# Diagonal copies onto ScalarE, one score buffer for all heads, scans cut at the chunks, and a new hand-written order for the four heads of an HGRN2 block

## The chip, the cores and the metric

The kernel runs on one core of a Trainium2 chip. The measure is device time in microseconds of one execution. Engines are named as in the profile: PE is TensorE (matmul), PEld its weight loads, DVE VectorE, ACT ScalarE, POOL GpSimd, SP SyncE (here only an issuer of DMAs). Each engine works through its own queue in the order in which the program was written out; semaphores make it wait for others.

## The reference

One decoder layer over 16 meta tokens and 1024 tokens, model width 1024, everything in float32. The mixer runs a gated linear recurrence (HGRN2, four heads of key and value width 128) beside a pooling branch; a gated MLP follows. Only the recurrence is touched by the change.

```python
def hgrn2(q, f_logit, i, g, lb, out_gain):
    f = lb + (1.0 - lb) * jax.nn.sigmoid(fl)
    log_f = jnp.log(jnp.maximum(f, LOG_FLOOR))
    k = (1.0 - lb) * jax.nn.sigmoid(-fl)
    ...
def _hgrn2_chunk_step(state, xs):
    b = jnp.cumsum(lf, axis=2)
    o_inter = jnp.einsum('bhtk,bhkv->bhtv', q * jnp.exp(b), state)
    diff = b[:, :, :, None, :] - b[:, :, None, :, :]
    decay = jnp.where(causal, jnp.exp(jnp.where(causal, diff, 0.0)), 0.0)
    scores = jnp.einsum('bhtk,bhtsk,bhsk->bhts', q, decay, k)
    o_intra = jnp.einsum('bhts,bhsv->bhtv', scores, v)
    ...
def reference(...):
    u = rmsnorm(h, mix_norm_pre[l])
    proj = u @ w_in[l]
    q, f_logit, i_in, g_out, v_pool, gate_a, gate_b = jnp.split(proj, cuts, axis=-1)
    a = hgrn2(q, f_logit, i_in, g_out, lbs[l], hgrn_out_norm[l])
    p = multiscale_pool(v_pool, pool_proj[l], pool_scale[l])
    z = (sigmoid(gate_a) * (a @ w_branch_hgrn[l]) + sigmoid(gate_b) * (p @ w_branch_pool[l]))
    h = h + rmsnorm(z @ w_out[l], mix_norm_post[l])
    ...  # gated MLP
```

The cumulative sum `b` starts anew at each chunk; the kernel uses chunks of 128 tokens behind a first one of 16 meta tokens.

## The kernel before

The time has four stretches. From 0 to about 250 us the input is normed and transposed and the merge gates are projected. From about 250 to 585 us come the heads, the pooling branch and the branch products (called the head stage here). Then come the output projection and the MLP, to the end at 1333 us.

**Arithmetic on PE.** A float32 matrix product is made from three products of parts: weights are cast to a high part (`whi`, ACT, L156) and the rest is subtracted into `wlo` (L157, on DVE or POOL). A projection job of the head stage (F the forget gate, Q the query, G the output gate, PV the pooling values, each for one head) is 72 matmuls of some 346 columns. BB and BA are the branch products of half that length.

**One head.** When F's product is there, ACT writes two sigmoids from PSUM (`post_f`, L629 and L630). Step c (`chain_f`) then makes the log gate: two ACT scalings (L634, L635), two DVE clamps (L636, L637), two ACT logarithms (L638, L639), an addition (`lf`, L640), and the cumulative sum `b` by a scan along 1040 columns (L641). The scan multiplies the running sum by `keep_on`, an array of ones with a zero at the start of each chunk. `head_steps` then runs in steps, one for each "h" in the order.

- Scores are made by levels 2, 4, 8, 16, 32, 64, two of them in a step. A level subtracts `b` from its middle value of each block (`sub`, L686), takes two exponentials on ACT (L688, L689), multiplies by `q` and by `kk` (`lq`, L690; `lk`, L691) into a tile `d`, and PE makes 32 or fewer small products into the PSUM tile `sl` (L708, or L702 for levels 32 and 64).
- Levels 2 to 16 go by a masked DVE copy (L724) into `dg`, a narrow array of 128 x 256, in which each group of 32 partitions holds its own 32 x 32 diagonal block of each of the 8 chunks. Levels 32 and 64 are copied by DVE straight into `sc`, the full score array of 128 x 1024 (L718).
- A later step makes the base of the diagonal blocks on PE (`sb`, L777), joins it into `dg` (L780), and copies the four groups of 32 partitions of `dg` onto the diagonal of `sc` (L788; `dg0` to `dg3`).
- Between them stand the decayed keys (`kd`: L745, L746, L750), the decayed queries (`qs`: L741, L751), the chunk decays `ebl` (L748), the products of odd steps (`e1q`, L758; `e1k`, L759), the transposes of `kd` (`pt`, L766, copied out by ACT at L767), the states (`ds`, L801; L804 on DVE) and the outputs (`po`).

**What sets the order.** `ORDER` is the sequence of jobs and steps written by hand: `F1` is a job, `Fa3` and `Fb3` its halves, `c1` the log gate chain, `h1` the next step of head 1, `sp`, `sa` and `w` splits and weight work. A scheduler then interleaves matmuls more finely within it. `POOLED` names the operations that POOL does instead of DVE (`lq32.1` is L690 of level 32 of head 1, `wQ0` the weight subtraction of job Q0), `ACTED` those that ACT does.

At the end of the head stage, DVE multiplies the gates into the branch products out of PSUM (L918), and `split_z` (L1172 to L1177) prepares the output projection, whose weights POOL splits at L1265.

Of the kernel before, what the change touches and what calls it, by code (L numbers as in the profile page):

```python
# [8 lines left out]
F32 = mybir.dt.float32  # L9
# [3 lines left out]
ALU = mybir.AluOpType  # L13

P = 128
D = 1024
SEQ = 1024
NM = 16
L = SEQ + NM
# [14 lines left out]
HEADS = 4  # L34
NCH = 8
# [8 lines left out]
BLK = 32  # L44
# [5 lines left out]
EARLY_G = 2  # L50
SUMS_AT = {5: (2,), 6: (2, 1), 8: (3,), 9: (1, 3), 10: (1, 4), 11: (4, 0), 12: (0, 0)}
FM_SLOTS = 26
LP = 1056
U0 = LP - L
NRAW = 3
ZA = 4
AHEAD = 3

ORDER = ("F0 c0 Q0 h0 F1 h0 h0 c1 Q1 h0 h1 h0 F2 h1 h1 c2 h0 h0 Q2 h1 h2 G2 h1 h0 h2 h0 Fa3 h1 h0 h1 h2 Fb3 h2 c3 "
# [3 lines left out]
POOLED = ("e1k.3 kdmul.2 kdmul.3 lk32.1 lk4.1 lq16.1 lq32.1 lq32.2 lq64.0 lq64.3 lq8.0 lq8.1 lq8.2 osg.2 sub2.2 "  # L63
          "sub32.1 sub8.1 wBA2 wBA6 wBA7 wBB2 wF0 wF2 wF3 wPP2 wPV0 wPV1 wQ0 wQ1 lq4.3 kdsub.1 qsmul.1 lk32.0 e1q.3 "
          "e1q.1 lq2.1 wQ2 sub2.3 rsl.0 lk32.3 qsmul.2 dg1.3").split()
ACTED = ("").split()
TRUNC = False

CH_ALL = [(0, 348), (348, 346), (694, 346)]
# [4 lines left out]
def trunk_kernel(ctx: ExitStack, tc: tile.TileContext, x, meta_tokens, mix_norm_pre,  # L74
# [4 lines left out]
    act, dve, pool_e, pe = nc.scalar, nc.vector, nc.gpsimd, nc.tensor  # L79

    cnt = [0]
    const = ctx.enter_context(tc.tile_pool(name="const", bufs=1))
# [21 lines left out]
    def slot(n, dtype=F32, name="s"):  # L104
        return stage["fm", "p"].tile([P, n], dtype, tag="fm", name=nm(name), padded_shape=[P, LP])

    def ubig(dtype, name, n=KD * LP):
        return upool.tile([P, n], dtype, tag="u", name=nm(name), padded_shape=[P, KD * LP])

# [13 lines left out]
    def small(shape, name, tag, bufs=4):  # L123
        return sm.tile(shape, F32, tag=tag, name=nm(name), bufs=bufs)
# [7 lines left out]
    open_pool("ps", 8, PSUM)  # L132


    eps_t = const.tile([P, 1], F32, name="eps_t")
    dve.memset(eps_t, EPS)
    act.activation(small([P, 1], "std", "ns"), eps_t, AF.Sqrt)
    ident = const.tile([P, P], F32, name="ident")
    make_identity(nc, ident)
    onesm = const.tile([P, P], F32, name="onesm")  # L140
    pool_e.memset(onesm, 1.0 / P)
    onesr = const.tile([P, P], F32R, name="onesr")
    pool_e.tensor_copy(onesr, onesm)
# [76 lines left out]
    class Strassen:  # L220
# [3 lines left out]

        ORDER = ("P1", "P2", "P6", "P5", "P3", "P7", "P4")
        MOVING = dict(P1="b11", P2="b21", P3="b22", P4="t4", P5="t1", P6="t2", P7="t3")
        SECOND = ("P3", "P5", "P7")

        def __init__(self, units, run, early, quarters, halo, put, whole):
# [6 lines left out]
            for u in run:  # L236
                self.seq += [(u, p) for p in self.ORDER if u >= early or p not in ("P1", "P2")]
            self.got, self.at, self.kept, self.begun = [], 0, [], {}
# [333 lines left out]
                dve.tensor_copy(um[:, :, NM:], rr(ulo[:, :, :NM]))  # L572

    vd = dram.tile([NCH, P, 512], F32, name="vscr")
    vmeta = const.tile([P, 512], F32, name="vmeta")

    um = slot(2 * NM * KD, F32R, "um").rearrange("p (k c) -> p k c", k=KD)
# [43 lines left out]
    def eng(op):  # L621
        return pool_e if op in POOLED else dve

# [9 lines left out]
    def chain_f(h, kk, b, f, f2):  # L633
        act.activation(f2, f, AF.Identity, scale=omlu[:, h : h + 1], bias=lbu[:, h : h + 1])  # L634
        act.activation(f, f, AF.Identity, scale=oml[:, h : h + 1], bias=lb[:, h : h + 1])  # L635
        dve.tensor_scalar(f2, f2, 1.0, LOG_FLOOR * LUP, ALU.min, ALU.max)  # L636
        dve.tensor_scalar(f, f, LSPLIT, None, ALU.max)  # L637
        act.activation(f2, f2, AF.Ln)  # L638
        act.activation(f, f, AF.Ln)  # L639
        eng(f"lf.{h}").tensor_tensor(f, f, f2, ALU.add)  # L640
        dve.tensor_tensor_scan(b, keep_on, f, 0.0, ALU.mult, ALU.add)  # L641
        heads[h].update(kk=kk, b=b, f=f)

    def post_q(h, pq):
# [5 lines left out]
    def head_steps(h):  # L650
        q, kk, b, lf = (heads[h][z] for z in ("q", "kk", "b", "f"))
# [2 lines left out]
                          vd[:, :, h * P : (h + 1) * P].rearrange("c p v -> p c v"))  # L654
        sc = slot(NCH * P, name="sc")
        scm, em = small([NM, 2 * HALO], "scm", "scm", 2), small([P, HALO * NM], "em", "em", 2)
        dg = small([P, NCH * BLK], "dg", "dg", 3)
        pool_e.memset(sc, 0.0)
        pool_e.memset(dg, 0.0)

# [81 lines left out]
        for t0, n, w in ((0, 1, NM), (NM, NCH, P)):  # L742
# [2 lines left out]
            eng(f"kdsub.{h}").tensor_tensor(kc, bc[:, :, w - 1 : w].to_broadcast([P, n, w]), bc, ALU.subtract)  # L745
        act.activation(kd, kd, AF.Exp)  # L746
        ebl = small([P, NCH], "ebl", "ebl", 2)
        dve.tensor_copy(ebl.rearrange("p (c t) -> p c t", t=1),  # L748
                        qs[:, NM:L].rearrange("p (c t) -> p c t", t=P)[:, :, P - 1 : P])
        eng(f"kdmul.{h}").tensor_tensor(kd, kd, kk, ALU.mult)  # L750
        eng(f"qsmul.{h}").tensor_tensor(qs[:, NM:], qs[:, NM:], q[:, NM:], ALU.mult)  # L751
# [10 lines left out]
        for j in range(2):  # L762
            pt = bank("pt")
            for i in range(4):
                t = NM + (4 * j + i) * P
# [8 lines left out]
        for c in range(NCH):  # L774
            for n in range(0, P, BLK):
                t = NM + c * P + n
# [42 lines left out]
        for j in range(2):  # L819
            ps = bank("po")  # L820
            for i in range(4):
                c = 4 * j + i
                t = NM + c * P
# [126 lines left out]
    BEGUN = [(e, p) for es in ((0, 1), (2, 3, UP0)) for p in ("P1", "P2") for e in es]  # L950
    KEPT = BEGUN + [(u, p) for u in (0, UP0) for p in Strassen.ORDER[2:]]
    kept = [[dram.tile([P, 1024], F32, name=f"kept{t}{h}") for h in "hl"] for t in range(len(KEPT) // 2)]
# [54 lines left out]

    order = ORDER.split()
    order = [(o_[:-1], int(o_[-1])) for o_ in order]
# [58 lines left out]
    with tc.manual_schedule(engines={E.Activation, E.DVE, E.PE}):  # L1068
# [77 lines left out]
        for e in range(0, EARLY, 2):  # L1146
            p = gates.start_pair(e)
# [4 lines left out]
    gates.finish()  # L1152
    close_pool("pf")
    open_pool("ps", 8, PSUM)

    keep_on = slot(L, name="keep_on")
    pool_e.memset(keep_on, 1.0)
    pool_e.memset(keep_on[:, NM:].rearrange("p (c t) -> p c t", t=P)[:, :, :1], 0.0)

    jobs_ = [(k.rstrip("a"), i) for k, i in order if k[0].isupper() and k[-1] != "b"]  # L1160
    branch = [o_ for o_ in jobs_ if o_[0] in ("BA", "BB")]
# [75 lines left out]
    for name, names in (("v1", ("b11h", "b11l", "b21h", "b21l")), ("v2", ("b22h", "b22l", "t1h", "t1l"))):  # L1237
        n, o = (HP, HO) if name == "v1" else (HN, 0)
        t = ubig(F32R, name)[:, : 16 * n].rearrange("p (i k t) -> p i k t", i=4, k=4)
# [505 lines left out]
    with tc.manual_schedule(engines={E.Activation, E.DVE}):  # L1745
        for s_ in range(3):
            banks = [[bank("pd") for _ in range(NT)] for _ in range(2)]
            for k in range(KH):
# [7 lines left out]
                if s_ == 2 and k in (1, 2):  # L1756
                    for t in range(NT):
                        c = (c21, c12)[k - 1][t]
# [64 lines left out]
```

## Time and profile before

| | |
|---|---|
| median of three runs | 1331.71 us (1331.02 to 1332.32) |
| the profiled execution | 1335.12 us, of which the span 1333.4 us |
| PE busy in the span | 1305.4 us (98%) |
| DVE, ACT, POOL busy | 972.5, 576.0, 437.3 us |
| granted clock, mean | 0.994 |
| head stage | about 250 to 585 us |

The profile comes from one execution, 1.7 us of which lie outside the span. PE is idle for 28 us of the span, so nearly every microsecond outside the matmuls' own time is a place where PE stands still, or where its clock is granted at half speed. A row of the windows view gives for a stretch the busy time of each engine with its instruction count, then the granted clock, the DMA share and the bandwidth.

### The profile page before, as it was taken

Reading aid. Unit: us, or ns where it says so; the run is one execution under the profiler, and the core shown is the slowest. Engines: PE = TensorE matmul, PEld = TensorE weight load, DVE = VectorE, ACT = ScalarE, POOL = GpSimd, SP = SyncE. Lnnn points to the kernel's source line nnn. Section 1 sums busy time; section 2 is a strip of 40 time slices with the busy share of each in tenths; the row PEclk is TensorE's granted clock in tenths of the full one; section 3 lists DMA queues with packets and bytes.
Section 4 is the critical chain, followed back from the end, with each engine's and each line's share of the span. In section 5 each row is a group of like instructions: output and inputs, shape, how many; then the busy total and the mean of one; then the engine's idle time right before and its main releaser. Section 6 shows DMA issues by size and latency. Waiting matters only on the chain.

```text
span 1333.4 us, 21871 instructions
## 1 busy us (share of the span) xinstructions
PE 1305.4 (98%) x8673; PEld 1157.9 (87%) x8673; DVE 972.5 (73%) x1234; ACT 576.0 (43%) x954; POOL 437.3 (33%) x335
## 2 busy tenths in 40 slices
PE   8999999998999999999999999999999999999997
PEld 7799899998889999977899888888888888888886
DVE  6765554269868987775678999888989985455757
ACT  5553333367556565235564222322222223454443
POOL 4015421226524620051026555546555652000000
PEclk9999999998999999999999999999999999999999
DMA  8134433321011157987686677776776799666644
GB/s 271 41 104 154 131 103 103 113 63 49 20 51 36 35 189 253 338 276 245 222 293 228 193 210 195 201 206 164 179 158 138 184 246 301 218 226 223 221 174 158
DMA packets 139672, 230.49 MB, mean 173 GB/s; under 512 B 9000, under 2 KB 77196, under 8 KB 139570
## 3 DMA queue, kind: packets, MB, share of 16 engines
q1 hardware_dynamic: 127506, 204.71, 46.2%
q0 software_dynamic: 12064, 24.38, 11.0%
q8 instruction: 68, 1.11, 0.3%
q14 instruction: 34, 0.28, 0.1%
HBM read 165.56 MB, written 86.53 MB: 189 GB/s over the span
## 4 chain that ended last, share of the span: by engine, by line
PE 84%; DVE 7%; ACT 3%; DMA 3%; issue 2%; SPq 0%; POOL 0%; DVEq 0%; ACTq 0%
PE P L313 15%; PE P L316 15%; PE P L314 15%; PE pd L190 5%; PE pd L191 5%; PE pd L192 5%; PE pm L190 2%; PE pm L191 2%; PE pm L192 2%; PE pv L191 1%; DVE d L686 1%; PE pv L192 1%; PE pv L190 1%; PE pq L210 1%; PE pq L211 1%
## 5 line engine op out<-in xcount | busy, mean ns | idle before, releaser
L314 PE MATMUL P<-v,whi 128*128 128x512 f32 (+2 forms) x408 | 140.7, 352 | 0.0
L313 PE MATMUL P<-v,whi 128*128 128x512 f32 (+2 forms) x408 | 140.7, 352 | 0.0
L316 PE MATMUL P<-v,wlo 128*128 128x512 f32 (+2 forms) x424 | 135.1, 349 | 0.0
L1557 DVE TENSOR_TENSOR rot<-wraw,rot 128x1024 fp32r<-128x1024 f32 x31 | 38.0, 1225 | 72.2 <-ACT rot L1556 72.2
L284 POOL TENSOR_TENSOR swa<-wraw,wraw 128x512 f32<-128x512 f32 x28 | 43.4, 1551 | 137.6 <-DMA wraw<-in_ffn_w_gate_dram 73.5
L313 PEld LDWEIGHTS P<-v,whi 128*128 128x128 f32 x408 | 76.7, 188 | 10.4
L314 PEld LDWEIGHTS P<-v,whi 128*128 128x128 f32 x408 | 76.6, 188 | 10.3
L258 ACT CAST whi<-wraw 128x512 fp32r<-128x512 f32 x78 | 46.0, 618 | 87.5 <-PE P L314 63.9
L316 PEld LDWEIGHTS P<-v,wlo 128*128 128x128 f32 x424 | 74.0, 188 | 10.8
L191 PE MATMUL pd<-rot 128*128 128x512 f32 x272 | 82.1, 389 | 0.0
L192 PE MATMUL pd<-rot 128*128 128x512 f32 x272 | 82.1, 389 | 0.0
L190 PE MATMUL pd<-rot 128*128 128x512 f32 x272 | 81.1, 390 | 0.1
L1556 ACT CAST rot<-wraw 128x1024 fp32r<-128x1024 f32 x31 | 32.7, 1055 | 90.8 <-PE pd L192 89.4
L259 DVE TENSOR_TENSOR wlo<-swb,whi 128x512 fp32r<-128x512 f32 x56 | 63.5, 1140 | 6.8 <-ACT whi L258 6.7
L258 ACT CAST whi<-swa 128x512 fp32r<-128x512 f32 x56 | 33.4, 618 | 81.2 <-PE P L314 78.3
L259 DVE TENSOR_TENSOR wlo<-wraw,whi 128x512 fp32r<-128x512 f32 x74 | 64.6, 895 | 2.9 <-ACT whi L258 2.9
L1485 DVE SCALAR_TENSOR_TENSOR y<-g,par,y 128x1024 f32<-128x1024 f32 x44 | 63.7, 1447 | 0.8
L258 ACT CAST whi<-swb 128x512 fp32r<-128x512 f32 x56 | 33.4, 618 | 69.4 <-PE P L314 65.0
L190 PEld LDWEIGHTS pd<-rot 128*128 128x128 f32 x272 | 51.1, 188 | 11.2 <-DVE p L1493 0.5
L192 PEld LDWEIGHTS pd<-rot 128*128 128x128 f32 x272 | 51.1, 188 | 10.7
L191 PEld LDWEIGHTS pd<-rot 128*128 128x128 f32 x272 | 51.0, 188 | 10.5
L313 PE MATMUL P<-t4h,whi 128*128 128x258 f32 (+1 forms) x196 | 57.0, 307 | 0.0
(425 smaller groups left out, 4103.9 us busy)
## 6 DMA issues: line engine op xcount, KB each, us to landing
wraw<-in_w_in_dram SPq DMA_DIRECT2D x36, 512.0 KB, 4.4
yt<-ysum SPq DMA_DIRECT2D x33, 512.0 KB, 4.6
wraw<-in_ffn_w_gate_dram SPq DMA_DIRECT2D x26, 512.0 KB, 8.5
wraw<-in_ffn_w_up_dram SPq DMA_DIRECT2D x22, 512.0 KB, 5.9
wsum<-in_ffn_w_down_dram SPq DMA_DIRECT2D x22, 512.0 KB, 9.3
wraw<-in_w_out_dram SPq DMA_DIRECT2D x18, 512.0 KB, 4.3
ysum<-ys SPq DMA_DIRECT2D x11, 768.0 KB, 7.5
sa<-sscr SPq DMA_DIRECT2D x16, 513.0 KB, 5.5
```

The lines of the kernel that those rows point to most:

```text
L190: pe.matmul(ps, ahi, bhi, start=first, stop=False)
L191: pe.matmul(ps, ahi, blo, start=False, stop=False)
L192: pe.matmul(ps, alo, bhi, start=False, stop=last)
L258: act.copy(hi, src)
L259: (pool_e if 4 <= i < 2 * self.early else dve).tensor_tensor(lo, src, rr(hi), ALU.subtract)
L284: pool_e.tensor_tensor(s1, a21, a22, ALU.add)
L313: pe.matmul(d, whi[:, k, :], xh[:, c : c + w], start=(k == 0 and onto is None), stop=False, **go)
L314: pe.matmul(d, whi[:, k, :], xl[:, c : c + w], start=False, stop=False, **go)
L316: pe.matmul(x[:, o : o + w], wlo[:, k, :], xh[:, c : c + w], start=False, stop=(k == 3), **go)
L1485: dve.scalar_tensor_tensor(a, g[:, j : j + SEQ], cvw[:, j, m : m + 1], a, ALU.mult, ALU.add)
L1556: act.copy(hi, src)
L1557: dve.tensor_tensor(lo, src, rr(hi), ALU.subtract)
```

## The change

- The 15 DVE copies onto the diagonal (L788) become ACT copies (L791 in the new file); the sixteenth, on POOL, is `dg2.3` instead of `dg1.3`. Two of head 3's copies of levels 32 and 64 go to ACT too, and the four `ebl` copies.
- The four `dg` tiles of a small ring of three become four parts of one slot, `dgs`.
- The scan over 1040 columns is nine scans, one of 16 columns and eight of 128, which start from 0.0 and multiply by a constant of ones. `keep_on` and its two POOL memsets go away. Another pool's length changes by 32 columns.
- `ORDER` is rewritten: F1 stands before Q0, Q1 and F2 and others are cut in halves. `POOLED` loses 13 operations (`e1k.3 e1q.3 kdmul.2 kdmul.3 lq2.1 lq32.1 osg.2 sub2.2 sub8.1 wF3 wPV0 wQ0 dg1.3`) and gains 13 (`dg2.3 e1k.1 kdsub.2 lf.0 lf.2 lk16.0 lk16.1 lk64.2 lq16.2 lq64.1 sub16.2 sub4.1 sub8.0`).

```diff
-LP = 1056
+LP = 1088
...
-ORDER = ("F0 c0 Q0 h0 F1 h0 h0 c1 Q1 h0 h1 h0 F2 h1 h1 c2 h0 h0 Q2 h1 h2 G2 h1 h0 h2 h0 Fa3 h1 h0 h1 h2 Fb3 h2 c3 "
+ORDER = ("F0 c0 F1 Q0 h0 Qa1 h0 h0 c1 Qb1 Fa2 h0 h1 h0 Fb2 h1 h1 c2 h0 h0 Q2 G2 h1 h2 Fa3 h2 h1 h0 h2 h1 h1 h0 h2 "
...
-ACTED = ("").split()
+ACTED = ("dg0.0 dg0.1 dg0.2 dg0.3 dg1.0 dg1.1 dg1.2 dg1.3 dg2.0 dg2.1 dg2.2 dg3.0 dg3.1 dg3.2 dg3.3 out64.3 out32.3").split()
...
+    ones = const.tile([P, P], F32, name="ones")
+    pool_e.memset(ones, 1.0)
...
-    onesm = const.tile([P, P], F32, name="onesm")
+    onesm = slot(P, name="onesm")
...
+    dgs = slot(HEADS * NCH * BLK, name="dgs")
...
-        dve.tensor_tensor_scan(b, keep_on, f, 0.0, ALU.mult, ALU.add)
+        for lo in range(NM - P, L, P):
+            t = slice(max(lo, 0), lo + P)
+            dve.tensor_tensor_scan(b[:, t], ones[:, : t.stop - t.start], f[:, t], 0.0, ALU.mult, ALU.add)
...
-        dg = small([P, NCH * BLK], "dg", "dg", 3)
+        dg = dgs[:, h * NCH * BLK : (h + 1) * NCH * BLK]
...
-        dve.tensor_copy(ebl.rearrange("p (c t) -> p c t", t=1),
+        act.copy(ebl.rearrange("p (c t) -> p c t", t=1),
...
-    keep_on = slot(L, name="keep_on")
-    pool_e.memset(keep_on, 1.0)
-    pool_e.memset(keep_on[:, NM:].rearrange("p (c t) -> p c t", t=P)[:, :, :1], 0.0)
```

Four places show how the rows of an engine's queue move. In these rows a line number and an operation are followed by the tile written, the tiles read and the shape; numbers behind a name tell tiles of one name apart. Line numbers of the changed file are three to five higher than those before.

On DVE, where head 0's log gate ends, before (`f_351` and `f_2641` are the two parts of the gate, `b_2640` its sums, `d` the level tiles of head 0):

```order
L637 TENSOR_SCALAR f_2641<-f_2641 128x1040
L640 TENSOR_TENSOR f_2641<-f_2641,f_351_2642 128x1040
L641 SCALAR_TENSOR_TENSOR b_2640<-keep_on_2537,f_2641 128x1040
L667 TENSOR_TENSOR em_2746<-b_2640 128x32
L686 TENSOR_TENSOR d_2750<-b_2640 128x1024
L686 TENSOR_TENSOR d_2756<-b_2640 128x1024
L669 TENSOR_TENSOR em_2746<-em_2746,kk_2639 128x32
```

The same place on DVE after the change:

```order
L640 TENSOR_SCALAR f_2641<-f_2641 128x1040
L646 SCALAR_TENSOR_TENSOR b_2640<-ones,f_2641 128x16
L646 SCALAR_TENSOR_TENSOR b_2640<-ones,f_2641 128x128 x8
L672 TENSOR_TENSOR em_2845<-b_2640 128x32
L674 TENSOR_TENSOR em_2845<-em_2845,kk_2639 128x32
L691 TENSOR_TENSOR d_2848<-b_2640 128x1024
L691 TENSOR_TENSOR d_2854<-b_2640 128x1024
```

The addition left for POOL, and one scan became nine.

On ACT, between the subtraction of head 0's first levels and head 1's logarithms, before (`f_2848` and `kk_2846` are head 1's gate and key, `d_2928` and `d_2934` head 0's levels 8 and 16; head 0's exponentials of levels 2 and 4 stand ahead of these rows):

```order
L629 ACTIVATE f_2848<-pf_2766 128x346
L630 ACTIVATE kk_2846<-pf_2766 128x346
L629 ACTIVATE f_2848<-pf_2767 128x346
L630 ACTIVATE kk_2846<-pf_2767 128x346
L676 COPY scm_2745<-sm_2856 16x4
L688 ACT_TABLE_LOAD
L688 ACTIVATE d_2928<-d_2928 128x64x8
L689 ACTIVATE d_2928<-d_2928 128x64x8
L688 ACTIVATE d_2934<-d_2934 128x32x16
L689 ACTIVATE d_2934<-d_2934 128x32x16
L634 ACTIVATE f_375_2849<-f_2848,lbu,omlu 128x1040
L635 ACTIVATE f_2848<-f_2848,lb,oml 128x1040
```

The same part of ACT's queue after the change (head 1's six sigmoids, into `f_2748` and `kk_2746`, stand five rows and more ahead of the first row shown):

```order
L652 ACTIVATE q_2837<-pq_2757,oml 128x342
L637 ACTIVATE f_362_2749<-f_2748,lbu,omlu 128x1040
L652 ACTIVATE q_2837<-pq_2758,oml 128x342
L693 ACTIVATE d_2848<-d_2848 128x256x2
L694 ACTIVATE d_2848<-d_2848 128x256x2
L693 ACTIVATE d_2854<-d_2854 128x128x4
L694 ACTIVATE d_2854<-d_2854 128x128x4
L638 ACTIVATE f_2748<-f_2748,lb,oml 128x1040
L693 ACTIVATE d_2974<-d_2974 128x64x8
L694 ACTIVATE d_2974<-d_2974 128x64x8
```

Head 1's gate chain (`f`) moved up, from behind all four levels of head 0 to between them.

On PE, where head 2's levels 8 and 16 (`d_3866`, `d_3872`) are used, before (`pf` is a product of job F3, `pt` the transposes of head 1):

```order
L214 MATMUL pf_3730<-uhi_88,wlo_3214 128x346
L214 MATMUL pf_3731<-uhi_88,wlo_3214 128x346
L708 MATMUL sl_3930<-d_3866 32x16 x32
L708 MATMUL sl_3972<-d_3872 32x16 x32
L766 MATMUL pt_4019<-ident,kd_3818 128x128 x4
L766 MATMUL pt_4025<-ident,kd_3818 128x128 x4
```

The two levels after the change (`d_3785` is level 8 and `d_3791` level 16 of head 2); "..." stands for 47 matmuls of projection jobs:

```order
L713 MATMUL sl_3751<-d_3602 32x16 x32
L707 MATMUL sl_3797<-d_3722 32x32 x16
L707 MATMUL sl_3816<-d_3728 64x64 x8
L782 MATMUL sb_3841<-q_2837,kk_2639 32x32 x32
L713 MATMUL sl_3879<-d_3785 32x16 x32
...
L799 MATMUL ds_4005<-vmeta,ktm_3749 128x128
L806 MATMUL ds_4008<-vh_2841,kt_3734 128x128 x4
L806 MATMUL ds_4017<-vh_2841,kt_3734 128x128 x3
L713 MATMUL sl_4040<-d_3791 32x16 x32
```

The two levels, which stood back to back, are now apart by more than half a projection job.

On DVE, head 0's copies onto the diagonal and what follows them, before:

```order
L724 COPY_PREDICATED dg_3487<-mask_146,sl_3657 128x64x2
L780 COPY_PREDICATED dg_2747<-mbase,sb_3691 128x256
L788 COPY sc_2744<-dg_2747 32x8x32 x4
L718 COPY sc_3069<-sl_3768 32x8x32 x2
L686 TENSOR_TENSOR d_3866<-b_3218 128x1024
L686 TENSOR_TENSOR d_3872<-b_3218 128x1024
```

On ACT, the copies after the change, with their neighbours (`whi_3951` is a weight of a job yet to come, `pf_3611` the first product of F3):

```order
L753 COPY ebl_3832<-qs_3826 128x8
L761 ACTIVATE e_461_3836<-f_2748 128x512
L762 ACTIVATE e_461_3836<-f_2748 128x512
L751 ACTIVATE kd_3827<-kd_3827 128x1040
L791 COPY sc_2843<-dgs_133 32x8x32 x4
L158 CAST whi_3951<-wraw_3949 128x1024
L632 ACT_TABLE_LOAD
L632 ACTIVATE f_3957<-pf_3611 128x348
```

The four copies moved from DVE, ahead of two subtractions of head 2, to ACT, ahead of a weight cast and of F3's sigmoids.

On SP, the first DMAs of the program, before (`row` is a tile of the input, `wiraw` the weights of the first projection):

```order
L456 DMA row_90<-in_x_dram 128x1024
L147 DMA g_7_92<-in_mix_norm_pre_dram 128x1024
L461 DMA wiraw_94<-in_w_in_dram 128x2x512
L456 DMA row_96<-in_x_dram 128x1024
L461 DMA wiraw_98<-in_w_in_dram 128x2x512
```

The first DMAs after the change (`wraw_749` is the weight that stood after the `prow` loads of parameters before, as row 20):

```order
L155 DMA wraw_749<-in_w_in_dram 128x8x128
L458 DMA row_92<-in_x_dram 128x1024
L149 DMA g_8_94<-in_mix_norm_pre_dram 128x1024
L463 DMA wiraw_96<-in_w_in_dram 128x2x512
L458 DMA row_98<-in_x_dram 128x1024
```

A weight of 512 KB moved to the head of the queue, and all input rows stand behind it.

More of the change, by code (lines that the diff above doesn't have):

```diff
@@ L57 @@
 AHEAD = 3
-ORDER = ("F0 c0 Q0 h0 F1 h0 h0 c1 Q1 h0 h1 h0 F2 h1 h1 c2 h0 h0 Q2 h1 h2 G2 h1 h0 h2 h0 Fa3 h1 h0 h1 h2 Fb3 h2 c3 "
[3 rows of a table removed]
-POOLED = ("e1k.3 kdmul.2 kdmul.3 lk32.1 lk4.1 lq16.1 lq32.1 lq32.2 lq64.0 lq64.3 lq8.0 lq8.1 lq8.2 osg.2 sub2.2 "
-          "sub32.1 sub8.1 wBA2 wBA6 wBA7 wBB2 wF0 wF2 wF3 wPP2 wPV0 wPV1 wQ0 wQ1 lq4.3 kdsub.1 qsmul.1 lk32.0 e1q.3 "
-          "e1q.1 lq2.1 wQ2 sub2.3 rsl.0 lk32.3 qsmul.2 dg1.3").split()
-ACTED = ("").split()
+ORDER = ("F0 c0 F1 Q0 h0 Qa1 h0 h0 c1 Qb1 Fa2 h0 h1 h0 Fb2 h1 h1 c2 h0 h0 Q2 G2 h1 h2 Fa3 h2 h1 h0 h2 h1 h1 h0 h2 "
[3 rows of a table added]
+POOLED = ("lk32.1 lk4.1 lq16.1 lq64.0 lq64.3 lq8.0 lq8.1 lq8.2 sub32.1 wBA2 wBA6 wBA7 wBB2 wF0 wF2 wPP2 wPV1 wQ1 "
+          "lq4.3 kdsub.1 qsmul.1 lk32.0 e1q.1 wQ2 sub2.3 rsl.0 lk32.3 qsmul.2 lf.0 lq64.1 lk64.2 e1k.1 sub4.1 lf.2 "
+          "lq16.2 kdsub.2 sub16.2 sub8.0 lk16.1 dg2.3 lq32.2 lk16.0").split()
+ACTED = ("dg0.0 dg0.1 dg0.2 dg0.3 dg1.0 dg1.1 dg1.2 dg1.3 dg2.0 dg2.1 dg2.2 dg3.0 dg3.1 dg3.2 dg3.3 out64.3 out32.3").split()
 TRUNC = False
```

6 rows, old and new, of the table ORDER are left out of this document.

## The prediction

> **What bounds the kernel now.** I read the page's busy times first, then the windows of the head stage, the waits of PE, the chain of waits at the longest stop and the timelines around it.
>
> ```profile
> PE 1305.4 (98%) x8673; PEld 1157.9 (87%) x8673; DVE 972.5 (73%) x1234; ACT 576.0 (43%) x954; POOL 437.3 (33%) x335
> ```
>
> The span is 1333.4 us, so PE stands still for 28.0 us. The matmuls' own work is the same in both kernels, so only this idle time and half-speed clock can be won. The windows view shows where they lie in the head stage (length, then busy us and instructions of PE, PEld, DVE, ACT and POOL, granted clock, DMA share, GB/s; windows without idle left out).
>
> ```profile
> 255.00:282.00 27.00, 27.00 (x173) 27.00 (x171) 14.43 (x14) 14.94 (x23) 6.54 (x3) 1.00 0.22 60
> 282.00:309.00 27.00, 26.37 (x410) 25.39 (x409) 17.48 (x18) 22.24 (x34) 10.78 (x6) 1.00 0.15 41
> 309.00:317.00 8.00, 2.61 (x165) 2.31 (x162) 8.00 (x6) 5.34 (x10) 7.21 (x4) 0.83 0.23 68
> 317.00:325.00 8.00, 8.00 (x49) 7.88 (x50) 6.47 (x10) 7.01 (x9) 3.86 (x3) 0.74 0.48 131
> 345.00:350.00 5.00, 3.04 (x142) 2.43 (x140) 2.84 (x6) 4.96 (x10) 0.00 (x0) 1.00 0.07 16
> 366.00:376.00 10.00, 6.64 (x108) 6.43 (x98) 6.77 (x11) 8.06 (x13) 2.74 (x1) 0.83 0.19 54
> 409.00:412.00 3.00, 1.58 (x73) 1.39 (x72) 2.20 (x4) 2.25 (x3) 0.28 (x1) 1.00 0.19 74
> 412.00:480.00 68.00, 67.15 (x712) 64.47 (x711) 63.95 (x66) 41.79 (x67) 38.06 (x18) 1.00 0.09 27
> 581.00:585.00 4.00, 1.01 (x4) 0.68 (x3) 3.97 (x5) 0.68 (x3) 2.94 (x2) 0.87 1.01 398
> ```
>
> PE idle is length less busy: 0, 0.63, 5.39, 0, 1.96, 3.36, 1.42, 0.85, 2.99, together 16.60 us. The first row also gives the pace of a projection job, 27.00 us for 173 matmuls, 0.156 each. Where PE waits long, DVE is full (8.00 of 8.00, 3.97 of 4.00), and the clock falls (0.83, 0.74, 0.83, 0.87). The waits of PE in the head stage name who released it:
>
> ```profile
> PE sl L708 <- DVE d L691: 4.8, 3, 3.4
> PE sl L702 <- DVE d L691: 1.8, 1, 1.8
> PE sl L702 <- DVE d L690: 1.7, 1, 1.7
> PE pf L210 <- ACT kt L767: 1.5, 1, 1.5
> PE sl L708 <- DVE d L690: 1.0, 1, 1.0
> ```
>
> The bound there is DVE's queue, ahead of a level's last multiplication. How the largest wait arises is in the chain of waits of 290 to 320 us (rows in between left out), and what lies ahead of it in the ACT timeline (the first row):
>
> ```profile
> 281.86 1.05 ACT L156 CAST whi<-wraw 128x1024 fp32r<-128x1024 f32 x1 [4.83 <-PE pf L211]
> 289.96 1.16 ACT f L634
> ...
> 295.78 1.25 DVE f L640
> 297.06 2.34 DVE b L641
> ...
> 305.99 2.23 DVE wlo L157
> 309.83 4.17 DVE d L690 x2
> 314.21 2.56 DVE d L691
> 316.90 1.94 PE sl L702 x16
> ```
>
> ACT stands 4.83 us until F1's product allows a cast to go; head 1's log gate starts at 289.96 only, its sums are there at 299.4, and then DVE needs 17 us for what stands ahead of the last level. Several of these operations last longer than their kind does alone. Two pairs of timeline rows (366 us, 581 us), the copies' shortest, median and longest in ns, their sum and one set of them show how:
>
> ```profile
> 366.59 2.82 DVE L691 TENSOR_TENSOR d<-d,kk 128x512 f32<-128x512 f32 x1
> 366.12 2.74 POOL L157 TENSOR_TENSOR wlo<-wraw,whi 128x1024 fp32r<-128x1024 f32 x1 [1.62 <-ACT whi L156]
> 581.46 2.30 DVE L1177 TENSOR_TENSOR zc<-sa,zc 128x2 fp32r<-128x2 f32 x1
> 581.37 2.36 POOL L1265 TENSOR_TENSOR wlo<-wraw,whi 128x1024 fp32r<-128x1024 f32 x1 [4.70 <-ACT whi L1263]
> L788 DVE COPY sc<-dg x15: 274/291/1980, 350.6 to 466.8; 32x256 f32<-32x256 f32 x15
> L788 DVE COPY sc<-dg 32x256 f32<-32x256 f32 x15 | 12.9, 863 | 0.3
> 350.59 2.91 DVE L788 COPY sc<-dg 32x256 f32<-32x256 f32 x4
> ```
>
> A subtraction of two columns took 2.30 us, and both DVE operations end just behind the POOL operation that runs beside them (369.41 behind 368.86, 583.76 behind 583.73): they waited for it. The copies are the same case, 0.29 us in the median and 0.86 in the mean.
>
> **The change part by part.** The sum is made against the profiled execution, 1335.12 us; its median lies 3.41 lower, at 1331.71, and the difference is taken over to that.
>
> *Load of the engines.* Prices are these rows and the medians above.
>
> ```profile
> L641 DVE TENSOR_TENSOR_SCAN b<-keep_on,f x4: 2324/2324/2325, 269.8 to 378.7; 128x1040 f32<-128x1040 f32 x4
> L667 DVE TENSOR_TENSOR em<-b x4: 178/193/956, 272.2 to 383.5; 128x32 f32<-128x32 f32 x4
> L718 DVE COPY sc<-sl x12: 405/422/683, 318.6 to 453.6; 32x256 f32<-32x256 f32 x8, 64x512 f32<-64x512 f32 x4
> L750 POOL TENSOR_TENSOR kd<-kd,kk 128x1040 f32<-128x1040 f32 x2 | 6.8, 3396 | 0.0
> L1172 ACT CAST zc<-sa 128x256 fp32r<-128x256 f32 x6 | 2.4, 402 | 6.1 <-DVE sa L1224 6.1
> ```
>
> The scan: no row shows a short one. From below, columns alone set the time and nine cost 2.33 like one; from above, each of eight more pays a whole small operation (0.178), 3.75. I take 3.6, near the upper end, since L667 shows that 32 columns already cost 0.178: 1.25 more per head, 5.0 in all. DVE loses 15 copies (15 x 0.29 = 4.4), three L718 (2 x 0.41 and 0.68: 1.5) and four `ebl` (as L667: 0.7), 6.6. By the operations that change between DVE and POOL it gains some 1.2 us (weights of three jobs, two L750, one L758 and one of 1026 columns come, two L640, L686, three L691 and one L745 go, 1.25 per full width, as L640 in the chain, and half of that per half). So DVE's own work changes by 5.0 - 6.6 + 1.2 = -0.4: nothing. POOL loses three weights, two L750, a half and one of 1026 columns, and gains two `lf`, one L686, three halves, one L745: at 3.4 for 1040 columns as L750, 2.5 for other full widths and 1.5 for halves (between L157's 2.74 and half of it) 18.3 against 16.3, some 2 less. ACT gains 15 copies at up to 0.40 (6.0), three L718 (1.4) and four small ones (0.8), 8.2, which it can hold as a whole (22.24 of 27.00 and 41.79 of 68.00 us busy in the rows), but not at each place. So no engine is relieved as a whole; what counts is order.
>
> *The stall of 309 to 317.* F1 stands ahead of Q0 now, so its product, and with it head 1's chain, is there a job (72 matmuls of 0.156, 11.2 us) earlier on PE. ACT puts the chain's scalings between head 0's exponentials. Of the 9.5 us in which DVE was idle from 282 to 309, part is thus used. Against it: the longer scan, and one more subtraction of head 1 on POOL (`sub4.1`) near 2.5 us, which its neighbours on DVE may wait out. DVE's rows from the first scan to the last level of this group lose one L640, two L686 and one L691 and gain an L690 and two long scans, 1.5 to 2.4 us less. Ends: nothing kept, or all 5.39 kept. I keep 2.0, since the lock-step with POOL stays: -3.4.
>
> *The stalls of 345 to 376* (1.96 + 3.36). Level 16 of head 2 had nothing between it and level 8 on PE; now 47 matmuls (47 x 0.156 = 7.3 us) cover it, more than the 3.36. And DVE's 2.91 us of diagonal copies from 350.59 no longer stand ahead of it. The wait for `kt` on ACT (1.5) I keep, as ACT has more to do: -3.8. Ends: all kept, since the copies are queued on ACT ahead of a weight cast and F3's sigmoids and hold both up until DVE has joined the blocks; or -5.3.
>
> *The clock.* 317 to 325 ran at 0.74: 8.00 x 0.26 = 2.1. 366 to 376 at 0.83 lost 1.7 at most, of which 0.3 fell on idle: 1.4. With the stalls shortened, -3.5. The Trainium skill, page "TensorE: Matmul & The Clock Gate", section "Why this matters for your kernels", asks for no gap above about 3 us between bursts. No wait in the rows of 309 to 317 is longer than 1.8 us, and yet the clock fell, so the measurement decides here: many short waits suffice. By that page's rule the clock after 317 would have stayed whole and 2.1 us less could be won, giving 1324.
>
> *409 to 581.* DVE is busy for 63.95 of 68.00 us, so what I computed as even load gives nothing; 1.42 + 0.85 kept. Ends: gone, or doubled.
>
> *The seam at 581* (2.99). It is a collision of POOL's weight split and a two-column subtraction, which the change doesn't touch by name; another phase may move it. Kept, with 0 and 4 as ends.
>
> *The start.* The first 512 KB weight now passes ahead of all rows of x. PE's first work hangs on the first of these, as the timeline of the start shows; the bandwidth of the first 20 us, in 40 slices, stands below it.
>
> ```profile
> 4.40 1.06 ACT L417 ACTIVATE un<-row 128x1024 f32<-128x1024 f32 x1 [2.10 <-DMA row<-in_x_dram]
> GB/s 0 0 0 90 90 336 344 402 287 238 229 266 406 438 430 418 381 406 401 406 389 377 393 393 406 406 418 401 426 410 410 401 393 418 393 295 205 262 377 410
> ```
>
> 512 KB at the 400 GB/s of most slices take 1.3 us, at the 288 GB/s of some 1.8. Ends 0 (the queues carry both loads side by side and the first row loses nothing) and 1.8; I take +1.3.
>
> Sum: -3.4 - 3.8 - 3.5 + 1.3 = -9.4, a profiled run of 1325.7 and a median of **1322 us**.
>
> **The Trainium skill against it.** Page "SBUF — State Buffer", section "SBUF: two separate sides", has the port pair of DVE and GpSimd as an exclusive lock for a whole instruction. The ends at 369.41 and 583.76 agree. It speaks against the change: by it the copies' waits are not removed with them but pass to the next DVE operation with two inputs, which is rival A's mechanism; the sum with all 12.9 us won would read 1314, by the page's rule 1322.
>
> **Rivals.**
>
> *A, relief only in part.* Of the copies' 12.9 us 8.5 are waits for POOL (12.9 - 15 x 0.29); they pass on to the next DVE operations, head 1's stall stays at 4 and the clock falls as before, or the gap at 366 comes back, now behind the ACT copies. For it: DVE full at 309 and 412. Against: 7.3 us of cover. Half of 10.7 comes back: -9.4 + 5.4 = -4.0, **1328 us**.
>
> *B, slower.* The chain before each head's levels grows: scan +1.25 for four heads, and `lf` on POOL for heads 0 and 2, up to 3.40 - 1.25 = 2.2 each. That is 9.4, all on PE's path if each head's levels wait for their sums, as head 1's did. With the old waits kept and the start, +10.7 at most; the scans alone and the start give 5.0 + 1.3 = 6.3, **1338 us**. It decides where a head's levels have less than 1.25 us to spare behind its sums, for `lf` less than 3.4; the 9.5 us of idle DVE in 282 to 309 speak against.
>
> *C, all goes.* No stall in 309 to 412 is left (5.39 + 1.96 + 3.36 + 1.42), nor the clock's 3.5, and the seam's 2.99 falls away: -18.6 + 1.3 = -17.3, **1314 us**. For it: only chance alignment makes the seam. Against: DVE remains as loaded.
>
> **How the numbers follow.** Chances: the forecast 0.55, A 0.17, B 0.16, C 0.12. A measurement tells 0.2% (2.7 us) from no change, 1329.0 to 1334.4. A reaches from 1325 to 1334 and gives half of its chance to no change: slower 0.16 + 0.01, same 0.08, faster 0.55 + 0.12 + 0.08. The range takes in C at its lower end and the unknown start, scan and seam at the upper: 1314 to 1334. The forecast's own range, with 2 us on the first stall, 2 on the seam and 1 on the start, is 1318 to 1327.
>
> **What would show it.** Right: the wait of `sl` for L691 and L690 falls from 9.3 to under 4, no window between 300 and 380 with a clock under 0.9, scans of some 3.6 us in sum per head, the first row 1 to 1.5 us later, DVE's busy time in the stage within 3 us of before. Wrong: a new wait of PE for a head's levels after `b`, a wait for ACT behind the copies, a second cluster at 410 to 480, or the seam elsewhere. What I can't see is how POOL's operations fall beside DVE's: each meeting is worth 1 to 2 us.

## The result

The changed kernel took 1314.72 us (median of four runs, 1313.35 to 1316.08) against 1331.8: a ratio of 0.9872, with a 95% interval of 0.9855 to 0.9889. That is 17.1 us less, where 9.7 were forecast. A ratio here is the one on record, against runs of the kernel before from the same series; it can differ by up to 0.2% from a median over 1331.8, and gains of whole kernels below go by the ratio. One execution each of two later kernels took 3313.69 and 7042.56 us, and isn't counted in their ratios. The profiled execution took 1314.41 us, with a span of 1312.7.

The page's busy times, of the changed kernel:

```profile
PE 1298.9 (99%) x8673; PEld 1156.5 (88%) x8673; DVE 950.8 (72%) x1243; ACT 582.3 (44%) x975; POOL 439.0 (33%) x335
```

PE stands still for 13.8 us instead of 28.0, and its own busy time is 6.5 us shorter with the same matmuls: that part is clock and pace. The head stage in windows, of the changed kernel, columns as before:

```profile
282.00:309.00 27.00, 26.96 (x437) 25.94 (x439) 21.19 (x30) 20.16 (x32) 14.24 (x7) 1.00 0.22 60
309.00:317.00 8.00, 6.32 (x198) 6.10 (x186) 7.96 (x11) 7.93 (x15) 3.69 (x3) 1.00 0.02 4
317.00:345.00 28.00, 28.00 (x255) 27.31 (x257) 21.86 (x34) 22.23 (x31) 13.63 (x7) 1.00 0.21 59
345.00:355.00 10.00, 9.63 (x399) 9.09 (x395) 8.16 (x9) 6.73 (x12) 10.00 (x7) 1.00 0.02 5
355.00:395.00 40.00, 40.00 (x424) 38.21 (x422) 29.70 (x48) 27.79 (x50) 20.05 (x11) 1.00 0.20 56
395.00:400.00 5.00, 4.05 (x157) 3.76 (x156) 2.65 (x4) 4.43 (x8) 2.43 (x2) 1.00 0.32 108
400.00:467.00 67.00, 67.00 (x715) 65.00 (x714) 53.22 (x60) 48.24 (x84) 32.63 (x16) 1.00 0.15 47
467.00:565.00 98.00, 98.00 (x630) 97.77 (x629) 73.83 (x122) 39.99 (x63) 6.62 (x5) 1.00 0.85 287
565.00:585.00 20.00, 20.00 (x90) 14.39 (x89) 14.98 (x12) 8.54 (x15) 15.66 (x11) 1.00 0.96 319
```

Idle is now 0.04, 1.68, 0.37 and 0.95, 3.04 us together up to the seam, and none at the seam; the granted clock is whole in every row. The waits of PE in the same stage, of the changed kernel:

```profile
PE sl L707 <- DVE dgs L729: 1.7, 2, 1.0
PE ms L838 <- ACT rh L891: 0.9, 1, 0.9
PE sb L782 <- issue: 0.4, 1, 0.4
```

No wait for a level's multiplication is left. The scans and the copies by tile (shortest, median and longest in ns), and the first row of x on ACT:

```profile
L646 DVE TENSOR_TENSOR_SCAN b<-ones,f x36: 190/397/2568, 271.0 to 372.1; 128x128 f32<-128x128 f32 x32, 128x16 f32<-128x16 f32 x4
L791 ACT COPY sc<-dgs x15: 388/403/408, 356.3 to 467.1; 32x256 f32<-32x256 f32 x15
7.09 1.06 ACT L419 ACTIVATE un<-row 128x1024 f32<-128x1024 f32 x1 [4.79 <-DMA row<-in_x_dram]
```

A scan of 128 columns takes 0.397 us, 3.4 us for a head (0.190 + 8 x 0.397). The copies take 0.403 us on ACT, all alike. The first row is 2.69 us later (7.09 against 4.40).

By stretches of the two profiled executions, taken at the first matmul of each part: the start costs 1.8 us (first projection at 11.33 instead of 9.56); from there to the first job F0 1.4 us are won; the head stage goes from 331.7 to 316.9 us (-14.9); the output projection from 105.4 to 99.6 (-5.8); and what follows is 0.5 shorter. Together -20.7, as the two profiled executions differ. The medians differ by 17.1; before's profiled execution lies 3.4 above its median, and the seam run below bears on that.

### The profile page after: what moved, and what is told of

It is laid out like the page before. It is cut to its first block, busy times and chain, and to the rows that moved or that the text cites. A ratio compares the mean times of both kernels' runs of the same rounds, so it can differ in the third digit from the quotient of the medians.

```text
span 1312.7 us, 21900 instructions
## 1 busy us (share of the span) xinstructions
PE 1298.9 (99%) x8673; PEld 1156.5 (88%) x8673; DVE 950.8 (72%) x1243; ACT 582.3 (44%) x975; POOL 439.0 (33%) x335
## 4 chain that ended last, share of the span: by engine, by line
PE 96%; ACT 1%; DVE 1%; DMA 1%; POOL 0%; issue 0%; SPq 0%; DVEq 0%
PE P L315 15%; PE P L316 15%; PE P L318 15%; PE pd L192 5%; PE pd L193 5%; PE pd L194 5%; PE pm L192 2%; PE pm L194 2%; PE pm L193 2%; PE ppv L212 1%; PE pv L192 1%; PE pv L193 1%; PE pbb L212 1%; PE ppv L216 1%; PE pbb L213 1%; PE pv L194 1%
```

## The experiments

Theory 1 was that the new order carries the gain. Theory 2, its first rival, was that the copies taken from DVE carry it. In the tables below "stage" is the head stage of the profiled execution, from the first matmul of F0 to the first of the output projection: 331.7 us before, 316.9 after.

### Order against the rest

All of the change but its order:

```diff
-ORDER = ("F0 c0 F1 Q0 h0 Qa1 h0 ...
+ORDER = ("F0 c0 Q0 h0 F1 h0 h0 ...      # and POOLED, as before
```

> All of the change but its order: the sequence of jobs and the list of POOL's operations are those of before. Theory 1 (the order carries the gain): the stalls of 309 to 317 and near 366 are back, with the longer scan and the late first row 1330 to 1335. Theory 2 (the copies that left DVE carry it): DVE has 12.9 us less to do and to wait for, stalls shrink, 1318 to 1322. Either way the first input row is late by 2.7 us, which costs about 2.

Only the order, in the kernel before:

```diff
-ORDER = ("F0 c0 Q0 h0 F1 h0 h0 ...
+ORDER = ("F0 c0 F1 Q0 h0 Qa1 h0 ...      # and POOLED, as after
```

> Before with the new sequence and the new list of POOL's operations and nothing else: the diagonal copies stay on DVE, the scan is one of 1040 columns with its mask, the first input row is first in the DMA queue. Theory 1 (order): 1312 to 1317, as the changed kernel less 2 us at the start. Theory 2 (copies): 1325 or more.

The changed kernel with the copies on DVE:

```diff
-ACTED = ("dg0.0 dg0.1 ... out64.3 out32.3").split()
+ACTED = ("").split()
-        act.copy(ebl.rearrange("p (c t) -> p c t", t=1),
+        dve.tensor_copy(ebl.rearrange("p (c t) -> p c t", t=1),
```

> The changed kernel with the diagonal copies, head 3's two copies and the four small ones back on DVE. Theory 1 (order): 1314 to 1318, DVE has room. Theory 2 (copies): 1323 or more, PE waits for levels again between 350 and 410.

Only the copies on ACT, in the kernel before (the same two edits the other way round, but with `dg2.3` on ACT in place of `dg1.3`, which POOL keeps here):

> Before with the 22 copies moved from DVE to ACT and nothing else. Theory 1 (order): 1328 to 1332, head 1's stall at 309 comes before the first diagonal copy and stays, the one at 366 shrinks at most by the 2.9 us of a set of copies. Theory 2 (copies): 1318 to 1322. By the port lock of the Trainium skill, page SBUF - State Buffer, section SBUF: two separate sides, the waits in the copies pass to the next DVE operation: no gain beyond 0.29 us a copy.

| kernel | median us | ratio to before | interval | stage us |
|---|---|---|---|---|
| changed | 1314.72 | 0.9872 | 0.9855 to 0.9889 | 316.9 |
| all but the order | 1343.94 | 1.0092 | 1.0072 to 1.0113 | 346.0 |
| order alone | 1321.14 | 0.9929 | 0.9914 to 0.9943 | 322.9 |
| all but the copies | 1315.86 | 0.9889 | 0.9870 to 0.9909 | 318.3 |
| copies alone | 1330.63 | 0.9982 | 0.9963 to 1.0001 | 334.0 |

The copies are worth nothing that these runs can tell, in either order; theory 2 falls. The order alone, that is the sequence together with the new list of POOL's operations, gives 0.71%, 9.5 us, less than expected. And the parts don't add: without the order the rest costs 12 us, where I had expected nothing, and with the order it gives some 7.6.

That the copies do nothing isn't for lack of relief. The windows view of the whole stage for four kernels, each in its own fence: before, changed, copies alone, all but the copies. The third busy time is DVE's.

```profile
248.00:580.00 332.00, 318.06 (x3379) 309.95 (x3379) 253.59 (x319) 187.69 (x294) 107.42 (x56) 0.98 0.38 121
```

```profile
248.00:565.00 317.00, 313.95 (x3380) 307.17 (x3379) 231.23 (x331) 194.00 (x316) 114.58 (x61) 1.00 0.39 127
```

```profile
248.00:581.00 333.00, 319.58 (x3371) 311.60 (x3371) 234.23 (x299) 195.98 (x317) 107.24 (x56) 0.97 0.38 122
```

```profile
248.00:566.00 318.00, 313.63 (x3376) 306.69 (x3375) 241.63 (x353) 189.40 (x296) 110.88 (x61) 1.00 0.39 127
```

With the copies alone moved, DVE's busy time in the stage falls by 19.4 us (253.59 to 234.23). By the prediction's prices 6.6 of them are the copies' own work; the rest is time by which operations lasted longer than alone. The kernel isn't faster all the same. Head 1's stalls from 309 to 317 come before the first copy onto the diagonal. The stall at 369 does have copies ahead of it. PE at that place, before:

```profile
369.46 1.05 PE L708 MATMUL sl<-d 128*32 128x16 f32 x64 [3.36 <-DVE d L691]
```

With the copies alone moved (two rows of PE, one of DVE, one of POOL):

```profile
366.27 0.74 PE L708 MATMUL sl<-d 128*32 128x16 f32 x64 [0.19 <-DVE d L691]
370.08 1.11 PE L766 MATMUL pt<-ident,kd 128*128 128x128 f32 x4 [2.49 <-DVE st L804]
366.13 2.87 DVE L759 TENSOR_TENSOR kk<-kk,e 128x512 f32<-128x512 f32 x1
366.10 2.36 POOL L157 TENSOR_TENSOR wlo<-wraw,whi 128x1024 fp32r<-128x1024 f32 x1 [1.04 <-ACT whi L156]
```

DVE is early enough for the level now, and that stall shrinks from 3.36 to 0.19 us. But POOL's weight subtraction, which lengthened a level's multiplication before (2.82 us at 366.59), meets DVE's next operation instead (L759, 2.87 us, where its three rows before took 0.68 to 0.69), and PE stands 2.49 us for what comes behind that. The wait moved to another operation rather than going away.

### The sequence without the new list of POOL's operations

> Before with the new sequence alone; the list of POOL's operations is the old one. If the sequence carries the gain of new_order_only (1321.1): 1319 to 1325. If the new split between DVE and POOL is needed with it: 1327 or more.

```diff
 # before, with this alone
-ORDER = ("F0 c0 Q0 h0 F1 h0 h0 ...
+ORDER = ("F0 c0 F1 Q0 h0 Qa1 h0 ...
```

It took 1328.37 us, 0.9961 (0.9945 to 0.9978), with a stage of 329.9. The sequence alone gives 5.2 us of the 9.5. The two longest waits of PE in the stage:

```profile
PE sm L674 <- DVE em L669: 4.8, 1, 4.8
PE sl L702 <- DVE dg L724: 1.7, 1, 1.7
```

Head 1's stall stays where it was (305 to 317, 6.4 us idle), only on another operation: DVE is busy for 11.90 of these 12 us. With the new list as well, which gives POOL `lf.0`, `sub8.0` and `sub4.1` among others, 1.3 us are left in the same 12 (the kernel with the order alone). So F1's early place isn't enough by itself; the distribution of the subtractions and additions has to change with it. What the new list would give without the sequence was not run, nor which of its operations count.

### What made the rest cost 12 us

> Before with the 22 copies on ACT and the nine scans, whose ones lie in the buffer of the old mask; the score buffers of the diagonal are still a ring of three. old_order, which has one buffer for all heads as well, took 1343.9, copies_act_only 1330.6. Theory N (the nine scans cost the difference, 0.9 us of DVE per head on PE's path): 1340 to 1344. Theory R (the one buffer for all heads does, which holds one of the 26 large buffers to the end): 1330 to 1333.

```diff
 # before, with the copies on ACT and
-        dve.tensor_tensor_scan(b, keep_on, f, 0.0, ALU.mult, ALU.add)
+        for lo in range(NM - P, L, P):
+            t = slice(max(lo, 0), lo + P)
+            dve.tensor_tensor_scan(b[:, t], keep_on[:, : t.stop - t.start], f[:, t], 0.0, ALU.mult, ALU.add)
...
-    pool_e.memset(keep_on[:, NM:].rearrange("p (c t) -> p c t", t=P)[:, :, :1], 0.0)
```

It took 1331.77 us, 0.9985 (0.9970 to 1.0001), with a stage of 335.7: no loss that can be told. The nine scans don't cost the 12 us. What is left between this kernel and the one with all but the order is the one buffer `dgs`, the place of the constants, the tiles of 1088 and the late start; the last two act outside the stage for the most part, and the stage is 10.3 us longer (346.0). From 400 to 430 us PE is idle for 8.3 us, against 2.2 with the ring of three. The waits of POOL between 380 and 480 us, of the kernel with all but the order, rows that name PE:

```profile
POOL d L691 <- PE ds L806: 5.5, 1, 5.5
...
POOL s L874 <- PE pt L774: 4.1, 1, 4.1
...
POOL s L874 <- PE po L829: 3.3, 1, 3.3
```

The subtraction that makes `d` doesn't read what the `ds` matmuls write, nor does a pooling sum read `pt` or `po`. The likely reason is that their output buffer is one that these matmuls still read. With the ring of three small buffers no such row stands in POOL's waits of that stretch. So the large buffers, of which `dgs` holds one until head 3 is through, while `keep_on` was given back after the last scan, are the likely cause; a run with `dgs` alone in the kernel before wasn't made. In the new order the stage gets shorter instead, from 322.9 us with the order alone to 316.9 with all of the change. Taking back one other part at a time doesn't undo that: 318.3 with the copies on DVE, 317.5 with one scan, 316.6 with the tiles of 1056 and the early start (the last two are below). By elimination the one buffer carries most of these 6 us, but it was never changed alone, and how it comes to help there isn't settled.

### Scan, log gate addition

The changed kernel with one scan of 1040 columns and its mask, and the changed kernel with the additions on DVE:

```diff
-        for lo in range(NM - P, L, P):
-            t = slice(max(lo, 0), lo + P)
-            dve.tensor_tensor_scan(b[:, t], ones[:, : t.stop - t.start], f[:, t], 0.0, ALU.mult, ALU.add)
+        dve.tensor_tensor_scan(b, keep_on, f, 0.0, ALU.mult, ALU.add)   # keep_on made as before
```

> The changed kernel with one scan of 1040 columns and its mask in place of nine. If a head's levels wait for its sums, 0.9 us a head come back: 1311 to 1313. If the order has given them slack: 1314 to 1316, same as the changed kernel.

```diff
-          "... rsl.0 lk32.3 qsmul.2 lf.0 lq64.1 lk64.2 e1k.1 sub4.1 lf.2 "
+          "... rsl.0 lk32.3 qsmul.2 lq64.1 lk64.2 e1k.1 sub4.1 "
```

> The changed kernel with the two log gate additions back on DVE instead of POOL (1.24 against 2.42 us each). If the sums are on PE's path: 1312 to 1313. If not, DVE only gets 2.5 us more to do: 1314 to 1316.

They took 1314.6 us (0.9872, 0.9857 to 0.9887) and 1315.08 us (0.9879, 0.9862 to 0.9895): both the same as the changed kernel. So the sums `b` have slack in the new order, and rival B's chain isn't on PE's path.

### The seam

```diff
 # before
-            pool_e.tensor_tensor(lo, raw, rr(hi), ALU.subtract)
+            dve.tensor_tensor(lo, raw, rr(hi), ALU.subtract)
             pool_e.dma_start(wlos[k], rr(lo))
```

> Before with the low part of the first output projection weights subtracted on DVE instead of POOL (eight operations, three of them before 600 us). Theory S (the seam's stall of 2.99 us and the half-speed clock behind it come from one two-column subtraction on DVE that waits for a POOL operation): the stall falls to about 1.2 us, the length of the subtraction now on DVE, or goes, and the clock stays whole: 1327 to 1329. Rival (the projection would wait there anyway for its first operands): 1331 to 1333, or longer.

The stall is gone, as the window in which PE goes over to the output projection shows in this kernel:

```profile
580.00:584.00 4.00, 4.00 (x20) 3.15 (x20) 3.67 (x9) 2.20 (x7) 0.00 (x0) 1.00 1.02 412
```

The output projection takes 100.8 us instead of the 105.4 of before's profiled execution, and yet the median is 1332.16, a ratio of 0.9995 (0.9985 to 1.0006). The theory named the collision rightly, as far as one execution goes, and its worth for the median wrongly. The two kernels with the copies on ACT and the old order, in which POOL still has this work, show output projections of 100.7 and 100.8 us too. The stall then most likely belongs to the one execution that was profiled rather than to the kernel, which fits its 3.4 us above the median. Two doubts stay: the head stage of this run is 1.4 us longer (333.2), so that much of a gain could be hidden, and whether other executions of before have the stall can't be seen. The longer stage has a place: from 366 to 376 us the granted clock reads 0.66 in this run and 0.83 before, with no more idle time (3.01 against 3.36 us).

### The start and the pace of PE

> The changed kernel with the tile of 1/128 in the constants again and the tiles 1056 long as before; the first weight then stands behind the input rows in the DMA queue as before. If the start costs what the shift of PE shows: 1.8 to 2.4 less, 1312.5. If a later wait takes it up: 1314 to 1315.

```diff
-LP = 1088
+LP = 1056
...
-    onesm = slot(P, name="onesm")
+    onesm = const.tile([P, P], F32, name="onesm")
```

It took 1316.23 us, 0.9883 (0.9868 to 0.9897): not faster, against an expectation of 1312.5 or 1314 to 1315, though the first row is there early again (ACT timeline of this kernel):

```profile
4.51 1.06 ACT L419 ACTIVATE un<-row 128x1024 f32<-128x1024 f32 x1 [2.21 <-DMA row<-in_x_dram]
```

Its PE follows that of before to within 0.05 us from 7 to 247 us, while the changed kernel starts 1.8 us late and makes up 1.4 of it on the way, without any idle time to win. So the changed kernel's matmuls are faster there. All kernels with tiles of 1088 showed this and all with tiles of 1056 did not, but the former also all started late. One run holds the start and changes the length, the other the reverse as far as the space allows:

```diff
 # the changed kernel
-LP = 1088
+LP = 1056
```

> The changed kernel with its tiles 1056 columns long as before instead of 1088; the late first input row stays. In the runs so far PE's projections between 20 and 248 us and the output projection ran 1% slower in every kernel with tiles of 1056 and an early first row, and 1% faster in every kernel with tiles of 1088 and a late one. Theory L (the length of the tiles, by where the operands lie): the slow pace is back with the late start, 2.0 and 1.0 us lost, 1317.5 to 1319. Theory D (the late start): pace and time as the changed kernel, 1314 to 1315.

```diff
 # the changed kernel
-LP = 1088
+LP = 1072
...
-    onesm = slot(P, name="onesm")
+    onesm = const.tile([P, P], F32, name="onesm")
```

> The changed kernel with the tile of 1/128 in the constants, so that the first input row is early again, and tiles of 1072 columns (as long as the space allows). Theory L: if 1072 has the good pace, 1312 to 1313; if only 1088 has it, 1316. Theory D (the pace comes with the late start): 1316, like start_back.

They took 1318.74 us (0.9884, 0.9862 to 0.9906) and 1317.4 us (0.9875, 0.9853 to 0.9896). These intervals overlap that of the changed kernel, but the matmuls tell the cases apart. The first row is late in the former and early in the latter, so it is the place of the constant `onesm` that moved it. One kind of projection matmul (512 columns) between 20 and 60 us, shortest, median and longest in ns, in the order before, changed, changed with 1056, changed with 1072 and an early start:

```profile
L190 PE MATMUL pv<-whi,uhi x32: 387/394/497, 21.5 to 59.8; 128*128 128x512 f32 x32
```

```profile
L192 PE MATMUL pv<-whi,uhi x33: 387/389/501, 19.7 to 59.6; 128*128 128x512 f32 x33
```

```profile
L192 PE MATMUL pv<-whi,uhi x31: 389/397/497, 20.2 to 59.3; 128*128 128x512 f32 x31
```

```profile
L192 PE MATMUL pv<-whi,uhi x32: 388/394/502, 19.6 to 59.4; 128*128 128x512 f32 x32
```

389 ns with tiles of 1088, 394 to 397 with 1056 and 1072, whatever the start: theory L holds and theory D falls. From the first projection matmul to F0 the four took 238.4, 237.0, 239.5 and 238.7 us, and the output projection 99.6 with 1088 against 100.7 and 100.8 with 1056 and 1072. So the length is worth 1.4 to 2.5 us in the first stretch and 1.1 in the output projection, about what the late first row costs. A version with both, 1088 and an early row, has no room in the space as it is divided and wasn't made, and none of the runs beats the changed kernel by more than can be told.

## Why the prediction was right, and where its sizes were off

The time, 1314.7, lies at the very edge of the range and next to rival C's 1314, not to the 1322 held likeliest. The direction was right, and so was the main mechanism: PE's idle time and its clock in the head stage, given back by the order. But the order alone carries only 9.5 of the 17.1 us. The rest came from parts that the prediction priced at nothing or at a loss, so the closeness to C's number is in part luck: C counted the seam, which most likely gave the median nothing, and had neither the pace of the longer tiles nor the gain that the order doesn't explain. Point by point:

- **"no engine is relieved as a whole; what counts is order".** The second half is shown: order alone 9.5 us, copies alone nothing to be told. It isn't all, though: with the order in place the other parts shorten the stage by 6.0 us more (322.9 to 316.9), for which the sum had no term. The first half failed: DVE's busy time in the stage fell by 22.4 us (253.59 to 231.23), where 3 had been allowed. With the copies still on DVE it fell by 12.0 of these (to 241.63), so more than half of the relief is not the copies'. POOL's rose by 7.2 (107.42 to 114.58), where 2 less had been computed. The prices were those of operations alone; how they fall beside each other is the likely reason for the rest, which was not split further. It mattered little, since DVE's average doesn't set PE's end.
- **The stall of 309 to 317, -3.4.** 1.68 us are left where 2.0 were kept. The size is right, the reason only in part: the sequence alone left 6.4 us idle there; the moves between DVE and POOL were needed with it, and I had booked one of them (`sub4.1`) as a cost. The 1.5 to 2.4 us less of DVE rows there comes to 1.3 by the prediction's own prices (three operations less at 1.25, two scans more at 1.25); it didn't enter the sum.
- **The stalls of 345 to 376, -3.8.** 0.37 us are left where 1.5 were kept. The wait for `kt` is gone. Of the two reasons given, the copies were not needed: with them back on DVE 0.6 us are left from 345 to 395.
- **The clock, -3.5.** All windows read 1.00. The stage won 14.9 us, of which idle time accounts for 10.9 (13.95 to 3.04); 4.0 are left for clock and pace. The size leans on one execution: with 2.68 us idle from 366 to 376 the clock reads 0.66 with the copies alone moved and 1.00 with all but the order.
- **409 to 581, kept.** This term failed: 2.6 us of idle time (2.27 as quoted, and 0.34 later) became 0.95. Together with the two above, the stage's idle time was under-sized by 3.7 us.
- **The seam, kept at 2.99.** In the profiled execution it fell away with the half-speed clock behind it, 4.7 of the output projection's 5.8. In the seam run its removal was worth nothing in the median. The step that failed is in the sum: it took over a stall of one execution, which lies 3.4 us above the median, as a part of the kernel, which it most likely isn't.
- **The start, +1.3.** The first row came 2.69 us later, the first projection 1.8. The sign was right, the size too small.
- **The tiles' length.** It had no term at all. It gave 1.4 us before the stage and 1.1 in the output projection, and so hid the start's cost.
- **Rival A's mechanism**, waits that pass to the next DVE operation, acts at single places and not in the sum. With the copies alone moved, the meeting with POOL at 366 passed from L691 to L759 and cost PE 2.49 us; over the stage DVE's busy time still fell by more than the copies' own work. The Trainium skill's page "SBUF — State Buffer", section "SBUF: two separate sides", has the pair of ports as a lock that one engine holds for a whole instruction while the other is blocked. The single pairs agree (ends at 583.76 and 583.73; at 366 a multiplication of 512 columns that takes 0.68 us elsewhere takes 2.82 or 2.87).
- **Rival B** would have needed `b` on PE's path. Going back to one scan and to additions on DVE left the time the same. The scans cost 3.4 us a head where I took 3.6.

In sum, of the profiled executions: stage -14.9 where -10.7 was forecast, start +1.8 for +1.3, pace -1.4, -1.1 and -0.5 for nothing; that makes -16.1, and the seam's 4.7 beyond that most likely belongs to one execution. The medians moved by 17.1.

## What to carry to other kernels

Busy time taken off an engine that PE waits for only at two or three places can be worth nothing, even where it stands ahead of one of those waits: 19 us less on DVE moved the time by less than could be told, since one stall wasn't behind the copies and the other came back behind the next operation that met POOL's. A better order with a fitting list of moved operations moved it by some 10. Parts of a change can depend on each other: what came with the order added 6 us of gain in the stage, and the same parts in the old order lengthened it by 14 (331.7 to 346.0), so a part measured alone, or argued alone, doesn't tell its worth. Before a stall of a profile is booked as a part of the kernel, see how that execution stands to the median: one that lies 3 us above it can hold a stall of 3 us that other executions don't have.

## What was not expected of the hardware

With the length of the tiles changed by 32 columns (from 1056 to 1088), projection matmuls of 512 columns became 1.3% faster (394 to 389 ns in the median of one kind), at a granted clock that reads 1.00 in all of them, and with 1072 they stayed at 394. The length sets the distance between the rows of operands and where all later buffers lie; which of these acts isn't settled.

A wait of PE late in the first 10 us had a price beyond itself: in the changed kernel, where PE stood for 2.06 us up to 9.70, the granted clock fell to 0.55 and 0.76 from 10 to 20 us, where before showed 1.00. All six kernels with the late first row show 0.50 to 0.74 from 10 to 15 us, and all eight with the early one 1.00. The windows of the changed kernel, and then the first of them before:

```profile
10.00:15.00 5.00, 4.86 (x14) 2.60 (x13) 3.82 (x7) 4.09 (x7) 2.31 (x7) 0.55 1.05 395
15.00:20.00 5.00, 5.00 (x22) 4.33 (x22) 4.66 (x6) 4.07 (x7) 0.00 (x0) 0.76 1.04 386
```

```profile
10.00:15.00 5.00, 3.55 (x16) 2.16 (x16) 4.47 (x8) 3.65 (x6) 4.38 (x13) 1.00 1.05 402
```

Yet PE's lag grew by no more than 0.6 us there, from 1.8 to 2.35, since before stood idle itself for 1.45 us of that window, at a whole clock.
